# SwiGLU over 8192 x 8192 float32: the stores issued by GpSimd instead of ScalarE

## Chip, cores, metric

One core of one Trainium2 chip. The metric is the device time of one execution in microseconds (us), median of several runs. Executions of the kernel before agree within 0.2%. In profile lines DVE is VectorE, ACT is ScalarE, POOL is GpSimd and SP is the sync engine; a q after a name (ACTq) is that engine's instruction queue.

## The reference

```python
def reference(x):                       # x: 8192 x 8192 float32
    a, b = np.split(x, 2, axis=-1)
    silu_b = b / (1 + np.exp(-b))
    return a * silu_b                   # 8192 x 4096 float32
```

268.4 MB are read and 134.2 MB written, with one activation and one multiplication per output element.

## The kernel before

Each of 32 tiles holds 256 rows of `x`: two rows (R = 2, 64 KiB) on each of 128 partitions. Three buffers rotate. SP issues the loads. ScalarE computes silu in place, VectorE writes the product over the front of the same buffer, and the store takes it from there. ScalarE issues the stores of tiles 0 to 29; the last two tiles' stores are on SP.

```python
    def load(i, rows=None):
        ...
        nc.sync.dma_start(
            out=tiles[i][:, lo * M : hi * M], in_=xv[i * P : (i + 1) * P, lo * M : hi * M]
        )

    def swiglu(i, k, c0=0, cw=half):
        ...
        nc.scalar.activation(out=b, in_=b, func=_SILU)
        nc.vector.tensor_mul(...)           # product over the front of the tile

    def store(i, c0=0, cw=R * half):
        (nc.scalar if i < last - 1 else nc.sync).dma_start(
            out=ov[i * P : (i + 1) * P, c0 : c0 + cw], in_=tiles[i][:, c0 : c0 + cw]
        )

    for i in range(BUFS):                   # BUFS = 3
        load(i)
    for i in range(last):                   # last = 31
        for k in range(R):
            swiglu(i, k)
        if i == last - 1:
            swiglu(last, 0)
        store(i)
        nxt = i + BUFS
        if nxt < last:
            load(nxt)                       # waits until store(i) has landed
        elif nxt == last:
            load(last, (0, 1))
            load(last, (1, 2))
    store(last, 0, half)
    for c0 in range(0, half, half // 2):
        swiglu(last, 1, c0, half // 2)
    store(last, half, half)
```

## Time and profile before

| | before |
|---|---|
| time | 936.18 us, median of 3 runs (936.04 to 936.34) |
| span of the profiled run | 934.8 us |
| bytes moved | 402.67 MB, 431 GB/s over the span |
| the 16 DMA engines busy | 99.8% |
| VectorE, ScalarE busy | 30%, 25% |
| a tile's compute | 12.6 us in every 29.0 us |

The groups of instructions show what the two compute engines wait for (after the bar: busy us, mean ns of one, then idle us before them and what ended it):

```profile
L51 DVE TENSOR_TENSOR xt<-xt 128x4096 f32<-128x4096 f32 (+1 forms) x65 | 283.3, 4359 | 637.7 <-ACT xt L50 634.5
L50 ACT ACTIVATE xt<-xt 128x4096 f32<-128x4096 f32 (+1 forms) x65 | 228.1, 3556 | 688.1 <-DMA xt<-in_x_dram 688.1
```

VectorE waits for ScalarE and ScalarE waits for loads, all 688.1 us of the idle time before its activations. It never waits for VectorE, although its queue holds each store until VectorE has finished that tile. The rest of the profile before is read in the prediction.

### The profile page before, as it was taken

How to read it: one execution, taken by the hardware profiler on the slowest of the kernel's cores; microseconds unless marked ns; L12 is line 12 of the kernel's file. 1: busy time of each engine (PE TensorE's matmuls, PEld its weight loads, DVE VectorE, ACT ScalarE, POOL GpSimd, SP SyncE). 2: the span in 40 equal slices, each digit the busy share in tenths (PEclk: the TensorE clock that was granted, in tenths of full speed). 3: DMA queues.
4: the chain of work that ended last, by engine and by line, in shares of the span. 5: the costliest groups of instructions: out<-in, count | busy, mean ns of one | idle time of the engine just before them, and what ended most of it. 6: DMA issues, size and time to landing. Idle time of an engine off the chain costs nothing.

```text
span 934.8 us, 367 instructions
## 1 busy us (share of the span) xinstructions
DVE 283.3 (30%) x65; ACT 229.4 (25%) x66; POOL 0.2 (0%) x4
## 2 busy tenths in 40 slices
DVE  0333312333123331133321333213332133331242
ACT  0223320233302333113331133311333203332041
POOL 0000000000000000000000000000000000000000
DMA  9999999999999999999999999999999999999998
GB/s 404 400 445 430 430 439 433 428 435 443 428 430 439 429 442 432 435 426 453 419 430 452 411 452 423 428 447 425 433 433 453 414 443 429 426 447 428 425 437 376
DMA packets 9506, 402.67 MB, mean 431 GB/s; under 512 B 1056, under 2 KB 1056, under 8 KB 1056
## 3 DMA queue, kind: packets, MB, share of 16 engines
q1 hardware_dynamic: 5184, 276.83, 68.6%
q10 hardware_dynamic: 4320, 125.83, 31.2%
q14 instruction: 2, 0.02, 0.0%
HBM read 268.44 MB, written 134.22 MB: 431 GB/s over the span
## 4 chain that ended last, share of the span: by engine, by line
DMA 84%; DVE 10%; ACT 4%; DVEq 0%; issue 0%; SPq 0%; ACTq 0%
DMA out_dram<-xt 42%; DMA xt<-in_x_dram 42%; DVE xt L51 10%; ACT xt L50 4%; DVEq L106 0%; SPq L43 0%; ACTq L50 0%; DVEq L51 0%
## 5 line engine op out<-in xcount | busy, mean ns | idle before, releaser
L51 DVE TENSOR_TENSOR xt<-xt 128x4096 f32<-128x4096 f32 (+1 forms) x65 | 283.3, 4359 | 637.7 <-ACT xt L50 634.5
L50 ACT ACTIVATE xt<-xt 128x4096 f32<-128x4096 f32 (+1 forms) x65 | 228.1, 3556 | 688.1 <-DMA xt<-in_x_dram 688.1
L50 ACT ACT_TABLE_LOAD x1 | 1.3, 1283 | 0.7 <-PEq L95 0.7
L95 POOL MEMSET const-bfloat16-1.0<- 128x1 bf16 x1 | 0.1, 103 | 0.0
L95 POOL MEMSET const-uint8-127<- 128x1 uint8 x1 | 0.1, 102 | 0.0
L95 POOL MEMSET const-float32-0.0<- 128x1 f32 x1 | 0.1, 100 | 0.2 <-issue 0.2
L95 POOL MEMSET const-float32-1.0<- 128x1 f32 x1 | 0.1, 99 | 0.0
## 6 DMA issues: line engine op xcount, KB each, us to landing
out_dram<-xt ACTq DMA_DIRECT2D x30, 4096.0 KB, 39.7
xt<-in_x_dram SPq DMA_DIRECT2D x2, 4096.0 KB, 27.1
out_dram<-xt SPq DMA_DIRECT2D x1, 4096.0 KB, 23.6
out_dram<-xt SPq DMA_DIRECT2D x2, 2048.0 KB, 14.5
xt<-in_x_dram SPq DMA_DIRECT2D x31, 34.5
```

The costliest lines, as they stand in the source:

```text
L50: nc.scalar.activation(out=b, in_=b, func=_SILU)
L51: nc.vector.tensor_mul(out=xt[:, k * half + c0 : k * half + c0 + cw], in0=xt[:, k * M + c0 : k * M + c0 + cw], in1=b,)
L95: nc = _bacc.Bacc("TRN2", target_bir_lowering=False, num_devices=1)
```

## The change

Intent: take issuing the stores off ScalarE's in-order queue and give it to GpSimd, which is otherwise idle. Descriptors for those 30 stores are then made in software.

```diff
     def store(i, c0=0, cw=R * half):
-        (nc.scalar if i < last - 1 else nc.sync).dma_start(
+        (nc.gpsimd if i < last - 1 else nc.sync).dma_start(
             out=ov[i * P : (i + 1) * P, c0 : c0 + cw], in_=tiles[i][:, c0 : c0 + cw]
         )
```

## The prediction

> **What bounds the kernel now.** I read the page first, then the chain of waits in order of time, then who waits for whom on the load queue, then DMA and engine time by stretch. The page gives compute and transfers:
>
> ```profile
> DVE 283.3 (30%) x65; ACT 229.4 (25%) x66; POOL 0.2 (0%) x4
> ...
> DMA  9999999999999999999999999999999999999998
> ...
> DMA packets 9506, 402.67 MB, mean 431 GB/s; under 512 B 1056, under 2 KB 1056, under 8 KB 1056
> ...
> q1 hardware_dynamic: 5184, 276.83, 68.6%
> q10 hardware_dynamic: 4320, 125.83, 31.2%
> ...
> out_dram<-xt ACTq DMA_DIRECT2D x30, 4096.0 KB, 39.7
> ```
>
> VectorE and ScalarE are idle 70% and 75% of the time. The 16 DMA engines are busy 68.6 + 31.2 = 99.8% of the span. Queue q10 is the one this change replaces: its 125.83 MB are the 30 stores of 4 MiB that ScalarE issues. It has 4320 / 30 = 144 packets per store, or 9 on each of 16 engines; 4320 / 9 = 480 of them are small (the page counts 1056 = 66 DMAs x 16 under 512 B), so 8 carry data on each engine, each one partition's row of 32 KiB. A load of 8.39 MB has the same count (5184 / 36 DMAs = 144), so its packets are 64 KiB.
>
> The chain that ended last repeats a cycle from the second tile on. Columns are start, length, what:
>
> ```profile
> 98.96 34.44 DMA xt<-in_x_dram
> 133.51 3.63 ACT xt L50
> 137.16 4.43 DVE xt L51
> 141.68 4.44 DVE xt L51
> 146.14 39.70 DMA out_dram<-xt
> 185.89 34.52 DMA xt<-in_x_dram
> ```
>
> It looks like a latency chain: load, compute, store, and the buffer's next load. But one turn takes 185.89 - 98.96 = 86.93 us and three buffers turn at once, so it moves three tiles, 3 x (8.389 + 4.194) = 37.75 MB, at 434 GB/s. A 4 MiB store alone at that rate would take 9.7 us and a load 19.3; they take 39.7 and 34.5 because they share the engines. The chain is long because the engines are full, not the other way round. The stretches agree (length, DVE, ACT, POOL, clock, DMA share, GB/s):
>
> ```profile
> 120.00:207.00 87.00, 26.55 (x6) 21.37 (x6) 0.00 (x0) 1.00 1.00 434
> 468.00:555.00 87.00, 26.55 (x6) 21.37 (x6) 0.00 (x0) 1.00 1.00 434
> ...
> 915.00:925.00 10.00, 4.50 (x2) 3.24 (x2) 0.00 (x0) 1.00 0.97 418
> 925.00:930.00 5.00, 0.00 (x0) 0.00 (x0) 0.00 (x0) 1.00 1.01 433
> 930.00:934.80 4.80, 0.00 (x0) 0.00 (x0) 0.00 (x0) 1.00 0.42 181
> ```
>
> All 402.67 MB at 434 GB/s are 927.8 us; the other 7.0 us of the span are the start, small dips and the last completion. That 7.0 us is all that any reordering can win.
>
> The load queue waits for stores to free buffers:
>
> ```profile
> SPq L43 <- DMA out_dram<-xt: 869.3, 29, 67.8
> ```
>
> This wait is not idle time of the engines, for two reasons. A load takes 34.5 us from issue to landing but one lands every 29.0 us, so each is issued 5.5 us before the one ahead of it has landed. A store takes 39.7 us, so each sits 10.7 us behind the store ahead of it on its queue. Both queues always hold work. The slice of 400 to 500 us has 492 packets on q1 (29.10 MB) and 492 on q10 (14.55 MB): the engines alternate packet for packet, and 64 KiB against 32 KiB is by luck the 2:1 that the kernel needs.
>
> **What the Trainium skill says.** "DMA: Bandwidth & Descriptors", section "Queues, rings and completion order": each DMA engine takes turns between its queues packet by packet. The trace agrees (492 against 492). The same page, section "Latency and other measured facts": the first byte takes about 0.6 us through the hardware path and about 1 us from GpSimd. The trace shows 0.34 us on ScalarE's sequencer for an issue; nothing here shows the GpSimd figure yet. The same page, section "Bandwidth": a 16 MB load issued from GpSimd moved at 425 GB/s, and the ceiling of the 16 ports is 435. This trace's 434 is already at that ceiling. "SBUF — State Buffer", section "Who interferes with whom": a DVE instruction with two SBUF inputs blocks GpSimd instructions that read SBUF, while descriptor generation needs the write side (the page marks this as inferred), so `tensor_mul` should not stop it. Not testable in this trace, where GpSimd does only 4 memsets.
>
> **The change part by part.**
> Removed: 30 issues of 0.34 us on ScalarE, 10.2 us of its queue, and its in-order wait for VectorE at each store. ScalarE spends 688.1 us waiting for loads, 20 to 22 us per tile, so the gain on the path is 0.
> Added: 30 issues on GpSimd, which does nothing else. Generating 128 row descriptors plus completions costs some time per store. From the two first-byte figures I take 0.4 us more than now; even 5 us would be out of sight, because a store already sits 10.7 us behind its predecessor. On the path: 0, except for the very first store at 35 us, when the loads of tiles 1 and 2 fill the engines anyway.
> Blocking by VectorE: a store is issued when its tile's two multiplications (8.96 us) have ended, and the next begin some 20 us later (29.0 - 8.96), so GpSimd has 20 us free in every period. Cost 0 with either reading of the port rule.
> Moved: 125.83 MB from a hardware queue to a software one. Bytes and engines stay. What can change is the rate of these bytes. If the rows stay whole (32 KiB per packet), nothing changes: +0. If the software path cuts rows or its rings cost something, my estimate is the skill's 425 against this trace's 434: 125.83 / 0.425 - 125.83 / 0.434 = 296.1 - 289.9 = +6.1 us.
> Unchanged: loads, and the last three stores, which are on SP. After the last load lands (914.5) the bytes left are those last stores, 8.39 MB, 19.3 us at 434; the end comes 20.3 us later, so the tail is full too and does not depend on GpSimd.
> Sum: +0 to +6 us, of which I take a little over a tenth of a per cent, +1, as most likely: **937 us**.
>
> **Rivals.**
> First, the share of the engines shifts. If the software packets are shorter, say 4 KiB (a guess), stores get 4 / 68 of the engines while a load is outstanding, so loads land in some 21 us and stores creep until the load ends. If several rows form one packet, it goes the other way. For it: the alternation by packets is in the trace. Against any effect on the time: whichever goes first, one buffer is in compute for 12.6 us at most while two others have some 29 us of transfers each, so the engines do not run dry. Time: 934 to 938. A new long wait of loads for stores could show without costing anything.
> Second, the software path is really slower: descriptors of 1 KiB or less, generation longer than 29.0 us per store, or rings whose fetches slow some of the engines, so that all wait for the slowest. For it: a DMA-bound kernel has no slack for this, as 1% on all bytes is 9 us. Against it: 425 GB/s at 16 MB in the skill, and rows of 32 KiB, which need few descriptors. A loss of 6% on the stores' rate alone would be 290 x 0.06 = 17 us, 954 us; a generation of 40 us per store would make the 30 stores alone last 1200 us.
> Third, it gets faster, because ScalarE no longer waits at stores. ScalarE's idle time ends at loads (688.1 us), never at VectorE, so this gives at most the odd microsecond of the 7.0 us over the floor: 932.
>
> **Range and chances.** Faster by over 2% means below 917.5 us, which is 402.67 MB at 439 GB/s, above both the measured 434 and the ceiling quoted: 1%. Slower by over 2% means above 954.9, which needs +18.7 us, three times my estimate for the software path: possible only with the second rival, 14%. The rest, 85%, within 2%. The range is skewed up for the same reason: 933 to 949.
>
> **What would show it right or wrong.** Right: q1 keeps 5184 packets and 276.83 MB; in place of q10 stands a software queue of 125.83 MB; DMA share stays 99% or more and 87 us stretches stay at 430 to 434 GB/s; ScalarE still waits only for loads; no issue shows on ScalarE's queue. Packets near 4320 and stores landing in about 40 us would show whole rows; many more packets with loads landing near 20 us would show the first rival. Wrong: a DMA share well under 99% in the middle slices (generation too slow, or engines waiting for the slowest), or a full share with GB/s under 425 (a costlier packet). If the stores' delay to the first byte exceeds 10 us, my 0.4 us is wrong, whatever the time does.

## The result, and the profile after

| | before | after |
|---|---|---|
| time, median | 936.26 us (4 runs, 936.04 to 936.64) | 935.94 us (4 runs, 935.75 to 936.30) |
| ratio, 95% interval | | 0.9997 (0.9979 to 1.0014) |
| span of the profiled run | 934.8 us | 934.3 us |

Executions over 1.5% slower than the fastest of the same kernel are left out of the means. Every ratio here is the mean time of one kernel's runs over that of the other's in the same rounds, so it is not quite the ratio of the medians quoted.

The time did not change. The page of the changed kernel shows that the stores did move:

```profile
DVE 283.3 (30%) x65; ACT 229.4 (25%) x66; POOL 16.3 (2%) x34
...
q1 hardware_dynamic: 5184, 276.83, 68.6%
q0 software_dynamic: 4320, 125.83, 31.2%
...
L58 POOL DMA_DIRECT2D out_dram<-xt x30 | 16.1, 537 | 854.8 <-DVE xt L51 854.8
...
out_dram<-xt POOLq DMA_DIRECT2D x30, 4096.0 KB, 40.5
...
xt<-in_x_dram SPq DMA_DIRECT2D x31, 33.5
```

A software queue of exactly 4320 packets, 125.83 MB and 31.2% stands in place of the hardware queue. The row of 32 KiB on each partition is still one packet. GpSimd spends 537 ns per store.

The last two lines give the median time from issue to landing. Stores take 40.5 us instead of 39.7, loads 33.5 instead of 34.5. The chain in order of time (start, length, what) shows how that balances:

```profile
99.11 33.15 DMA xt<-in_x_dram
132.36 3.62 ACT xt L50
136.01 4.44 DVE xt L51
140.54 4.44 DVE xt L51
145.26 40.74 DMA out_dram<-xt
186.05 33.47 DMA xt<-in_x_dram
```

The second multiplication ends at 144.98, and the store is issued at 145.26, 0.28 us later (before: 0.02 us). It also takes about 1 us longer to land than before, and the load takes about 1 us less. One turn is 186.05 - 99.11 = 86.94 us; before it was 86.93. The extra microsecond of the store is repaid within the turn, because both transfers share full engines. A stretch of the middle says the same (length, DVE, ACT, POOL, clock, DMA share, GB/s):

```profile
120.00:207.00 87.00, 26.55 (x6) 21.37 (x6) 1.60 (x3) 1.00 1.00 434
```

Full share and 434 GB/s, as before.

### The profile page after: what moved, and what is told of

Its sections match the earlier page's. It is cut to its first block, busy times and chain, and to the rows that moved or that the text cites. A ratio compares the mean times of both kernels' runs of the same rounds, so it can differ in the third digit from the quotient of the medians.

```text
span 934.3 us, 400 instructions
## 1 busy us (share of the span) xinstructions
DVE 283.3 (30%) x65; ACT 229.4 (25%) x66; POOL 16.3 (2%) x34
## 3 DMA queue, kind: packets, MB, share of 16 engines
q0 software_dynamic: 4320, 125.83, 31.2%
## 4 chain that ended last, share of the span: by engine, by line
DMA 84%; DVE 10%; ACT 4%; issue 1%; DVEq 0%; SPq 0%; ACTq 0%
DMA out_dram<-xt 43%; DMA xt<-in_x_dram 40%; DVE xt L51 10%; ACT xt L50 4%; DVEq L106 0%; SPq L43 0%; ACTq L50 0%; DVEq L51 0%
## 5 line engine op out<-in xcount | busy, mean ns | idle before, releaser
L51 DVE TENSOR_TENSOR xt<-xt 128x4096 f32<-128x4096 f32 (+1 forms) x65 | 283.3, 4359 | 636.9 <-ACT xt L50 633.7
L50 ACT ACTIVATE xt<-xt 128x4096 f32<-128x4096 f32 (+1 forms) x65 | 228.1, 3556 | 687.3 <-DMA xt<-in_x_dram 687.3
L58 POOL DMA_DIRECT2D out_dram<-xt x30 | 16.1, 537 | 854.8 <-DVE xt L51 854.8
## 6 DMA issues: line engine op xcount, KB each, us to landing
out_dram<-xt POOLq DMA_DIRECT2D x30, 4096.0 KB, 40.5
xt<-in_x_dram SPq DMA_DIRECT2D x31, 33.5
```

What stands on the lines that cost most here:

```text
L51: nc.vector.tensor_mul(out=xt[:, k * half + c0 : k * half + c0 + cw], in0=xt[:, k * M + c0 : k * M + c0 + cw], in1=b,)
L58: (nc.gpsimd if i < last - 1 else nc.sync).dma_start(out=ov[i * P : (i + 1) * P, c0 : c0 + cw], in_=tiles[i][:, c0 : c0 + cw])
```

## The experiments

The theory to test: the full DMA engines set the time, the software path moves the same packets at the same rate, and its later start hides behind a backlog of transfers. The backlog is the time that a transfer spends queueing behind the one ahead of it. The rivals: the software path costs nothing at all, so nothing is hidden; it moves bytes more slowly and something offsets that; or the load-compute-store chain sets the time, and the result is neutral only because GpSimd issues as quickly as ScalarE. All twelve kernels gave correct results.

### The cost of a software-issued store, with nothing to hide it

One buffer and a plain loop, so that every store is alone on the engines:

```diff
-    BUFS = 3
+    BUFS = 1
...
-        (nc.gpsimd if i < last - 1 else nc.sync).dma_start(
+        nc.gpsimd.dma_start(                # control: nc.scalar
...
+    for i in range(ntiles):
+        load(i)
+        for k in range(R):
+            swiglu(i, k)
+        store(i)                            # in place of both loops and the tail
```

> One buffer in place of three, a plain loop, every store issued by GpSimd. Nothing overlaps, so every microsecond of issue and completion is on the path. Main theory (the software path has a small fixed cost that three buffers hide): about 32 x (21.5 load + 12.6 compute + 12 store) = 1475 us, and 32 x 0.5 to 1 us = 16 to 32 us more than the same kernel with hardware-issued stores. Rival (the software path costs nothing at all, so there is nothing to hide): within 5 us of the hardware form. Rival (stores move more slowly on the software path): over 50 us more.

> The control of the one-buffer kernel: the same loop, stores issued by ScalarE. About 1450 us by all theories; only the difference from the GpSimd form counts.

Measured: 1484.84 us from GpSimd and 1467.68 us from ScalarE, both above the sums expected; only their difference was to count. The difference is 17.2 us, or 17.2 / 32 = 0.54 us per store. The chains show where it lies. First GpSimd:

```profile
446.98 4.43 DVE xt L51
451.41 0.28 issue
451.70 11.36 DMA out_dram<-xt
```

Then ScalarE:

```profile
443.31 4.44 DVE xt L51
447.74 0.02 issue
447.76 11.14 DMA out_dram<-xt
```

From the end of the multiplication to the store's issue it is 0.28 us against 0.02, and from issue to landing 11.36 against 11.14. Together that is 0.48 us, close to the 0.54 from the times. So the software path has a fixed cost, and the "nothing to hide" rival falls. In the changed kernel the three buffers make ten turns, so 0.54 us left on the path of each would add some 5 us; the interval measured there ends at +0.14%, or 1.3 us.

### The rate of the software path, on two thirds of the bytes

```diff
-        nc.sync.dma_start(                  # in load
+        nc.gpsimd.dma_start(
...
-        (nc.gpsimd if i < last - 1 else nc.sync).dma_start(
+        (nc.scalar if i < last - 1 else nc.sync).dma_start(
```

> The software path for the loads instead of the stores: 268 MB, in 64 KiB rows, issued by GpSimd; stores on ScalarE as before. Main theory (rate and packets are the same on both paths): 934 to 939 us, packet count 144 per load on the software queue. Rival (the software path moves bytes some 2% more slowly, hidden for stores by something): +1.4%, 945 to 955 us, as two thirds of the bytes are on it.

Measured: 941.76 us, ratio 1.0057 (1.0042 to 1.0072). That falls between the two expectations, so the stretches must decide:

```profile
468.00:555.00 87.00, 26.55 (x6) 21.37 (x6) 1.58 (x3) 1.00 1.00 434
...
925.00:930.00 5.00, 1.88 (x1) 3.71 (x2) 0.00 (x0) 1.00 0.61 262
930.00:935.00 5.00, 2.62 (x2) 0.00 (x0) 0.00 (x0) 1.00 0.37 157
```

The middle runs at 434 GB/s with 268 MB on the software queue. The rate rival falls: a slower path would show there. The time is lost at the end, where the engines idle while the last half row is computed. The last load landed at 926.18 us, against 914.5 in the kernel before. In this version the last loads and the last stores are on different queues and share the engines, while before they followed each other in SP's queue.

### All stores on GpSimd, and its control

```diff
-        (nc.gpsimd if i < last - 1 else nc.sync).dma_start(
+        nc.gpsimd.dma_start(                # control: nc.scalar
```

> The last three stores too are issued by GpSimd. Main theory: the end is full of stores, so this moves only the order at the end: store 30 no longer waits behind the last load in SP's queue, shares the engines with it, and the last load lands later, up to 3 us; 935 to 941 us. Rival (the software path has a cost that the changed kernel avoids by leaving the last stores on SP, such as a long completion): over 945 us.

> The kernel before with the last three stores on ScalarE too: the hardware form of the run in which GpSimd issues all stores (940.65 us). If the 4 us lost there come from the order at the end (the last stores on a queue other than the last load's), this form loses them as well: 939 to 941 us, with the same idle gap of the DMA engines while the last half row is computed. If they come from the software path: 936 to 937 us.

Measured: 940.65 us from GpSimd (ratio 1.0047, 1.0030 to 1.0064) and 936.44 us from ScalarE (1.0001, 0.9984 to 1.0018). The first agreed with my expectation. The control did not: I expected the loss in both. The stretch from 925 to 930 us, first GpSimd:

```profile
925.00:930.00 5.00, 4.49 (x2) 1.88 (x2) 0.09 (x1) 1.00 0.38 164
```

and ScalarE:

```profile
925.00:930.00 5.00, 1.96 (x1) 0.00 (x0) 0.00 (x0) 1.00 0.90 380
```

The middle stretches of the GpSimd form are at 434 GB/s, so its loss is in the end alone. The timelines show a difference that I had overlooked. In the program, `swiglu(last, 0)` stands before `store(30)`, and ScalarE works in order. It therefore issued store 30 only at 904.85 us, after the activation that waits for the last tile's first half; GpSimd issued it at 899.84, as soon as the product was ready. The earlier store shares the engines with the last load, which landed at 923.2 instead of 920.5, and the last store went out at 929.91 instead of 926.99. The end is 3.9 us later.

```profile
899.84 0.53 POOL L58 DMA_DIRECT2D out_dram<-xt  x1 [28.47 <-DVE xt L51]
```

```profile
904.83 3.62 ACT L50 ACTIVATE xt<-xt 128x4096 f32<-128x4096 f32 x1 [9.79 <-DMA xt<-in_x_dram]
904.85 8.42 ACTq L58 DMA_DIRECT2D out_dram<-xt  x2
```

The first view is of the GpSimd form, the second of the ScalarE form (a timeline merges issues that follow each other: x2). So 2.9 us of the 3.9 us were already there when the last store was issued; the remaining 1.0 us is not explained. That the early issue of store 30 causes this is read from the timelines, not shown: the run that would show it (ScalarE issuing store 30 ahead of `swiglu(last, 0)`) was not made. What is shown: leaving the last stores on SP, as the change does, avoids a loss of 4 us that comes when GpSimd issues them.

### Delaying the store's issue on purpose

Before each store GpSimd copies 8 columns of the finished tile, so that it has to wait for it, and then fills a scratch tile n times, n = 4, 8 or 12:

```diff
+    dpool = ctx.enter_context(tc.tile_pool(name="delay", bufs=1))
+    scr = dpool.tile([P, 2048], x.dtype, name="scr")
...
+        if i < last - 1:
+            nc.gpsimd.tensor_copy(
+                out=scr[:, 0:8], in_=tiles[i][:, R * half - 8 : R * half]
+            )
+            for _ in range(4):              # 8, 12
+                nc.gpsimd.memset(scr[:], 0.0)
         (nc.gpsimd if i < last - 1 else nc.sync).dma_start(
```

> As the changed kernel, but GpSimd does about 8 us of other work (one copy of 8 columns that waits for the tile, then 4 fills of a scratch tile of 128x2048) before it issues each store. Main theory (the engines always hold a backlog; a store sits some 10.7 us behind its predecessor, so a late issue isn't seen): 934 to 938 us. Rival (the load-compute-store chain sets the time, and the change was neutral only because GpSimd issues as fast as ScalarE): 8 us per turn of the chain, 10 turns, 1010 to 1020 us.

> Eight fills, some 15.3 us on GpSimd before each store, between the 7.9 us that cost 2 us and the 23 us that cost 73. The backlog behind which a store hides is 40.5 - 29.0 = 11.5 us at most (4.19 MB at a third of 434 GB/s take 29.0 us, and stores landed in 40.5). Main theory: 4 us are past the backlog, so loads are issued some 4 us later but still before their predecessors have landed (5.5 us): 936 to 945 us. Rival (the loss grows in proportion to the delay past 8 us): some 970 us.

> The same with 12 fills, about 24 us before each store. Main theory: beyond the 10.7 us of backlog but still under the 29.0 us that a tile takes, so the engines stay busy most of the time: 935 to 960 us. Rival (chain): 24 us per turn, 10 turns, some 1170 us. If the delay comes out over 29 us GpSimd itself is the bound, 30 x delay.

| fills | store issued after the product | time | ratio (95%) |
|---|---|---|---|
| 0 (the change) | 0.3 us | 935.94 us | 0.9997 (0.9979 to 1.0014) |
| 4 | 7.7 us | 938.94 us | 1.0025 (1.0010 to 1.0040) |
| 8 | 15.2 us | 971.18 us | 1.0378 (1.0362 to 1.0393) |
| 12 | 22.6 us | 1009.4 us | 1.0776 (1.0758 to 1.0794) |

The second column is read from one store in each timeline; with 4 fills the product below ends at 428.77 + 8.95 = 437.72, and the issue is at 445.44:

```profile
428.77 8.95 DVE L53 TENSOR_TENSOR xt<-xt 128x4096 f32<-128x4096 f32 x2 [20.19 <-ACT xt L52]
...
445.44 0.53 POOL L66 DMA_DIRECT2D out_dram<-xt  x1
```

The first delay settles the chain rival. An additional 7.4 us in each of ten turns would be 74 us; measured are 2.3 us over the kernel before. The time from issue to landing of a store (minimum, median, maximum) with 4 fills:

```profile
DMA to landing us min/median/max: 12.9/33.7/33.9
```

In the changed kernel the median was 40.5. The store goes out 7.4 us later and needs 6.8 us less, so it lands at nearly the same moment: the time was spent queueing behind the store ahead. The little that is lost is lost early:

```profile
120.00:207.00 87.00, 26.55 (x6) 21.38 (x6) 22.63 (x19) 1.00 0.99 421
207.00:294.00 87.00, 26.55 (x6) 21.37 (x6) 23.36 (x17) 1.00 1.00 428
294.00:381.00 87.00, 26.55 (x6) 21.37 (x6) 24.92 (x20) 1.00 1.00 434
```

From 294 us on the rate is 434 GB/s again.

The two longer delays refuted my expectations (936 to 945, and 935 to 960). Past the backlog of 11.5 us (40.5 measured less the 29.0 that 4.19 MB take at a third of 434 GB/s) the delay costs. With 8 fills the stores go out 14.9 us later than in the changed kernel, 3.4 us more than the backlog; the loss of 34.9 us over ten turns is 3.5 us per turn, so all of the excess stays on the path. With 12 fills the excess is 10.8 us and the loss 72.7 us, 7.3 per turn, about two thirds of it. With 8 fills the 30 delayed stores land in 28.2 us at the median, just under 29.0, so little queueing is left:

```profile
out_dram<-xt POOLq DMA_DIRECT2D x30, 4096.0 KB, 28.2
```

Two of its stretches:

```profile
381.00:468.00 87.00, 24.16 (x6) 19.98 (x6) 45.30 (x30) 1.00 1.01 419
468.00:555.00 87.00, 24.46 (x6) 16.59 (x6) 45.30 (x30) 1.00 0.96 407
```

The rate falls to 407 to 422 GB/s while the engines' busy share stays at 96 to 101%. The pages split it: the two queues' packets take 98.7% of a span of 968.7 us, or 956 us, against 99.8% of 934.3, or 932. So 24 us of the 34 show as packets that take longer and the rest as idle engines. Why packets take longer is left open.

### Shorter packets on both paths

Each store is cut into two DMAs of interleaved pieces, of 4 KiB (f = 1024) or 512 B (f = 128):

```diff
+        o = o.rearrange("p (b a f) -> p b a f", a=2, f=1024)    # f=128
+        t = t.rearrange("p (b a f) -> p b a f", a=2, f=1024)
+        for h in range(2):
+            nc.gpsimd.dma_start(out=o[:, :, h, :], in_=t[:, :, h, :])   # control: nc.scalar
```

> Each store cut into two DMAs of interleaved pieces of 4 KiB (512 pieces each), issued by GpSimd. Packets of stores are 8 times as many and 8 times as short. Main theory: generation takes under 29 us per tile, so no loss from it; short packets give the loads a larger share (loads land near 22 us), the time moves by the packets' own cost only: 936 to 945 us, and the same as its hardware control within 1%. Rival (software generation is per piece and slow, over 15 ns a piece is still hidden: 1024 x 15 ns = 15 us): a loss over 2% against the control.

> The control of the kernel with 4 KiB pieces: the same two DMAs per store, issued by ScalarE. All theories: 936 to 945 us; the shift of share to the loads should show here as well, if arbitration is by packets.

> Stores in pieces of 512 B: two DMAs of 4096 pieces each per store, issued by GpSimd. This asks whether software generation can become the bound. At 4 KiB GpSimd was busy 0.71 us per 512 pieces against 0.53 for 128, about 0.5 ns a piece, so 2.5 us per DMA here: hidden. Main theory: short packets cost both forms alike, within 1% of the hardware control, both well over 950 us. Rival (the busy time understates generation): the GpSimd form is over 5% slower than its control, with GpSimd busy most of each period.

> The control with pieces of 512 B, issued by ScalarE. At 4 KiB the pair stood at 953 us. All theories: slower than that, 980 to 1100 us, because a packet of 512 B carries an eighth of the bytes for the same overhead and gives loads nearly the whole of the engines while they last.

| pieces | from GpSimd | from ScalarE |
|---|---|---|
| rows of 32 KiB (the change, before) | 935.94 us | 936.26 us |
| 4 KiB | 953.71 us, ratio 1.0179 (1.0154 to 1.0204) | 953.37 us, 1.0181 (1.0161 to 1.0200) |
| 512 B | 1096.28 us, ratio 1.1710 (1.1692 to 1.1727) | 1120.31 us, 1.1967 (1.1949 to 1.1985) |

At 4 KiB the two paths cost the same, and both cost more than I expected. The shift of share is there: from GpSimd, loads land in 25.9 us at the median instead of 33.5. I had put the effect of such a shift at 934 to 938 us. It is 953. No run separates the shorter packets' own cost from the shift, but the pages say which is the larger: from GpSimd the store packets take 32.3% of 950.8 us, or 307.1, against 31.2% of 934.3, or 291.5. These 15.6 us are nearly all of the 16.5 us that the span grew, and the shares of the two queues add up to 100.5%, so nothing points to engines that run dry. (Packet times overlap in part, so this is a reading and not a proof.)

At 512 B I expected the two within 1%, and the control between 980 and 1100 us; it took 1120. GpSimd's form is the faster by 24 us. The queues' packets show one possible reason, first from GpSimd at 4 KiB:

```profile
q0 software_dynamic: 31680, 125.83, 32.3%
```

From GpSimd at 512 B:

```profile
q0 software_dynamic: 31680, 125.83, 36.0%
```

From ScalarE at 512 B:

```profile
q10 hardware_dynamic: 246720, 125.83, 37.5%
```

The issues themselves (ns, minimum, median, maximum), from the view of the output tensor's instructions, first GpSimd:

```profile
L66 POOL DMA_DIRECT2D out_dram<-xt x60: 1644/1644/1772, 35.5 to 1032.6; - x60
```

then ScalarE:

```profile
L66 ACTq DMA_DIRECT2D out_dram<-xt x60: 541/10998/29670, 35.4 to 1062.8; - x60
```

The software path has as many packets at 512 B as at 4 KiB: it puts eight pieces into one packet. The hardware path makes one packet of each piece. And an issue holds ScalarE's queue for 11.0 us at the median and up to 29.7 us, while one on GpSimd takes 1.64 us. (The shortest on ScalarE took 0.54 us, so the number of pieces alone does not make it long.) In ScalarE's timeline two issues end at 451.69 us, and the next activation starts at 451.87, though a load issued at 425.37 would have landed by 448.2 at the median of 22.8 us. Packing and the held queue would both favour GpSimd; no run takes them apart. By the pages, store packets take 36.0% of 1092.7 us, or 393, from GpSimd and 37.5% of 1118.8, or 420, from ScalarE: 26 us, which is as much as the whole difference.

Software generation did not become the bound. The busy time of GpSimd was 0.54 us per DMA of 128 pieces, 0.72 us for 512 (43.2 / 60) and 1.65 us for 4096, 9% of the span in all. One more thing appeared: at 512 B the second DMA of a store often started about 19 us after the first, though its data were ready. The profile puts 20 such waits down to the landing of a load (20.3 us each on average); why is not explained by these runs.

No version beat both kernels. With whole rows 402.67 MB at 434 GB/s leave 7 us of the span to win, and no experiment touched them.

## Why the prediction was right, point by point

It put the time at 937 us (933 to 949); it was 935.94.

- **The bound.** Right: both kernels move 434 GB/s in the middle at full share, and a turn is 86.93 and 86.94 us. That this is the engines' doing, not the chain's, was argued from the backlog and is now shown: 7.4 us of delay per turn cost 2.3 us in all. The 492 packets on each queue, though, did not show that the engines take turns packet by packet, as the prediction said: a load and a store have 144 packets each here, and equal numbers follow from that alone. The run with 512 B pieces from ScalarE shows the turns: from 430 to 445 us, while a load is outstanding, 97 packets of the loads' queue (6.36 MB) start and 80 of the stores' (0.04 MB).
- **ScalarE freed: 0, and the third rival.** Right: its idle time still ends at loads (687.3 us after, 688.1 before).
- **Start of a store, 0.4 us later.** Slightly low: 0.54 us per store, measured with one buffer. Hidden, as said. "Even 5 us would be out of sight" holds: 7.4 us is all but hidden; 14.9 us is not.
- **Blocking by VectorE: 0.** The multiplications take the same (283.3 us in both), and the store starts 0.28 us after the last one. As the prediction said, the two hardly overlap, so no run here tests the port rule for descriptor generation.
- **Rate of the software path: +0 to +6, taken as +1.** It is 0 for whole rows: 4320 packets and 434 GB/s, even with the loads on that path. The single figure of 425 GB/s for one large transfer should not have been carried over to a stream of overlapping ones.
- **The full tail, independent of GpSimd.** Right for this change, and by the program's order: with the last stores on GpSimd the time was 4 us worse, and with the loads there 5 us.
- **First rival, a shifted share that costs nothing.** The step was wrong in size, though not needed: the packets stayed whole. With 4 KiB packets the shift appeared and the time was 953 us, not 934 to 938. By the pages, what it left out is the shorter packets' own time (15.6 us), not engines that run dry. For delays "the engines do not run dry" was too simple: past the backlog of 11.5 us all of the excess (8 fills) or two thirds of it (12 fills) counts.
- **Second rival.** It failed as judged. The slow case of 40 us of generation per store did not show even at 8192 pieces per store.

## What to carry to other kernels

Before moving an issue to another engine, ask whether a transfer queues behind another of its kind: time from issue to landing longer than the period says so, and the excess is an estimate of the delay that may be added at little cost (here 7.4 us of 11.5 cost 0.25%). Compare packet counts and GB/s before and after: here, with full DMA engines, both stood and so did the time. Look at the order of the last loads and stores separately, as it moved the end by 4 to 5 us here, and keep rows long: 4 KiB pieces cost 1.8% and 512 B pieces 17 to 20%, whichever engine issued them.

## What the Trainium skill lacked or had wrong

- "DMA: Bandwidth & Descriptors", section "SWDGE vs HWDGE vs iDMA", calls a packet preferably at most 4096 B and at most 64 descriptors. The runs agree for short pieces (31680 packets from GpSimd with 512 B as with 4 KiB) but show a row of 32 KiB as one packet (4320). It does not say that the hardware path left 512 B pieces unpacked here: 246720 packets.
- The same page, section "Issuing engines are not separate DMA queues", calls the issue time that another engine saves usually small relative to the DMA itself. With 512 B pieces it was not: 11.0 us at the median on ScalarE, where the DMA landed 30.1 us after its issue, against 1.64 us on GpSimd.
- The same page, section "Latency and other measured facts", has about 1 us against 0.6 us to the first byte. No page gives the difference per whole store: 0.54 us of time, 0.26 us of it before the issue shows in the profile.
- The same page, section "Bandwidth", has 425 GB/s for a single 16 MB transfer from GpSimd. It gives none for a stream of overlapping loads on that path: 434 GB/s here.
